# Whole fp32 operands in the experts' one-hot matmuls, and an overflow loop that prepares each block one block ahead

## The chip, the cores and the metric

The kernel runs on one core of a Trainium2 chip. The metric is the time of one execution on the device in microseconds. Times of a kernel are compared as medians of several runs; the profile shows one more execution, with every instruction of the five engines: PE (TensorE, matmuls; its weight loads are shown apart as PEld), DVE (VectorE), ACT (ScalarE), POOL (GpSimd) and SP (SyncE, which here issues nearly all DMAs).

## The reference, cut to what matters

The trunk has two layers. Each mixes 512 tokens of width 1024 by three mixers, attends to 256 memory tokens, and ends in a mixture of 32 experts, of which each token takes two:

```python
def hierarchical_moe(x, ...):
    g_p, g_idx = lax.top_k(softmax(t @ w_group + b_group), 1)
    e_p, e_idx = lax.top_k(softmax(e_logits[token, g_idx]), 2)
    weights = g_p * e_p / sum(e_p)
    expert_id = g_idx * 8 + e_idx
    gate = sum(one_hot(expert_id, 32) * weights)
    for e in range(32):
        h = silu(t @ w_gate[e]) * (t @ w_up[e])
        out = out + (h @ w_down[e]) * gate[:, e:e + 1]
    return out
# x = layer_norm(ALPHA * x + hierarchical_moe(x, ...), ln3_g, ln3_b)
```

All values are fp32. The change touches only the mixture of experts.

## The kernel before

The tokens lie in four tiles of 128 (t = 0 to 3). An expert has 64 slots (CAP), and experts are worked in pairs p = 0 to 15, so a pair fills 128 rows. Only the tokens that chose a pair's experts are worked: a one-hot matrix with a 1 where a token has a slot picks them.

**Two forms of an fp32 matmul.** A matmul whose operands are fp32 as they stand is compiled to two instructions on PE, which the trace shows as two records. An operand that `split` (L355 to L357) has cut into a high and a low half of type fp32r (ACT copies the high half, DVE subtracts it to get the low one) is multiplied by one record for each half. A one-hot matrix needs no low half.

**Router.** `router_tile` (L1158) runs once for each token tile at the end of the memory attention's output projection: layer norm, transposes, logits (L1178, L1179), the choice of experts on DVE (L1182 to L1199), then the split of the tile into the two halves X[0], X[1] (L1201 to L1205), the rank of each token among those of its expert (PE L1207 to L1209, the last of them needing the DVE result `rM` of L1199), its slot (DVE L1211 to L1214) and the one-hot rows of the first two pairs (L1219, L1220). Four more matmuls (L1251) serve the gates.

**First gather.** `gather_first` (L1329) gathers the tokens of pairs 0 and 1: for each tile t and each of eight column blocks f, two matmuls of 256 columns (L1340), one for each half. Later pairs get their tokens from DRAM by an indirect DMA (`fetch` on POOL) and eight transposes (`fetched`, L1325).

**The loop over pairs** in `moe` (L1421). Each turn issues on PE, by hand-written order, first the `down` matmuls of the pair before (L1395) and the `up` matmuls of this one (L1372), both with whole fp32 operands of 64 columns each, and then four pieces, each made of transposes for the next pair (L1325, in the first two pieces), token tables (L1304) or the turn of the hidden values (L1385), followed by two calls of `scatter`. `scatter` (L1513) adds a pair's results to the tokens: for each tile t and half of the width hf two matmuls of 512 columns (L1518), with the two halves y[0] and y[1] of the result, and one DVE addition (L1522). y[0] is made by ACT (L1397) from the down product, y[1] by DVE (L1398). So a pair has 8 calls of `scatter` and 16 records. There are 16 sets of scatter in a layer: the first, while pair 1 is under way; 14 in the later turns; and one in the tail.

**The tail.** After the last pair its two halves of down and scatter follow, now with sums for the last norm (L1524). In layer 0 filler matmuls of the next layer (tile `fb`, L393 to L395) are mixed in.

**Overflow.** Tokens beyond an expert's 64 slots are worked in blocks by a loop whose count is known only at run time (L1564, L1565). Here it runs no block in layer 0 and one block in layer 1. In a block, POOL compares all slots (L1538, eight instructions), adds (L1539) and PE finds the tokens (L1542), the weights (L1549) and the transposed one-hot rows (L1554); POOL then fetches the tokens by an indirect DMA (L1315), PE transposes them (L1325), and up (L1581), down (L1594) and scatter (L1603, DVE L1604) follow. SP loads the block's weights (L1571). After the loop comes `last_norm` (L1616).

## Time and profile before

| what | value |
|---|---|
| median of 3 runs | 1554.85 us (1550.07 to 1559.25) |
| the profiled execution's own time | 1561.04 us |
| its span in the trace | 1559.24 us |
| PE busy | 1478.3 us, 95% of the span |
| DVE busy | 1054.6 us, 68% |
| ACT busy | 592.0 us, 38% |
| POOL busy | 88.3 us, 6% |
| scatter matmuls L1518 | 512 records, 153.4 us |
| first gather L1340 | 128 records |
| read from HBM | 307.88 MB |

A row of a timeline gives the start, the duration, the engine, line and operation, tile names, the shape (rows x columns), and how many like instructions it stands for; brackets hold the idle time before it and what ended that. Matmuls overlap in the pipeline, so the spacing of starts is the price of a matmul in a stream, not the duration of one. Durations are those of the one profiled execution.

### The profile page before, as it was taken

Reading aid. Unit: us, or ns where it says so; the run is one execution under the profiler, and the core shown is the slowest. Engines: PE = TensorE matmul, PEld = TensorE weight load, DVE = VectorE, ACT = ScalarE, POOL = GpSimd, SP = SyncE. Lnnn points to the kernel's source line nnn. Section 1 sums busy time; section 2 is a strip of 40 time slices with the busy share of each in tenths; the row PEclk is TensorE's granted clock in tenths of the full one; section 3 lists DMA queues with packets and bytes.
Section 4 is the critical chain, followed back from the end, with each engine's and each line's share of the span. In section 5 each row is a group of like instructions: output and inputs, shape, how many; then the busy total and the mean of one; then the engine's idle time right before and its main releaser. Section 6 shows DMA issues by size and latency. Waiting matters only on the chain. (4 is left out here: it accounts for less than half of the span.)

```text
span 1559.2 us, 22997 instructions
## 1 busy us (share of the span) xinstructions
PE 1478.3 (95%) x8646; PEld 1011.7 (65%) x8646; DVE 1054.6 (68%) x2316; ACT 592.0 (38%) x1137; POOL 88.3 (6%) x102
## 2 busy tenths in 40 slices
PE   8999999999998999999799999999999999999984
PEld 6788876788785344444578878658887844444432
DVE  6868678576467986454856867786664699755454
ACT  6544346425333232332463342562442333323212
POOL 0000000010000011110000000000000011111010
PEclk9999899999999999999899999999999999999996
DMA  6432220413437999996533322014225589999931
GB/s 227 143 129 82 89 75 21 167 63 108 138 126 273 414 412 413 413 411 279 171 128 109 110 102 75 28 66 158 82 95 174 203 332 413 413 413 413 411 136 55
DMA packets 95909, 314.53 MB, mean 202 GB/s; under 512 B 12820, under 2 KB 13332, under 8 KB 95668
## 3 DMA queue, kind: packets, MB, share of 16 engines
q1 hardware_dynamic: 90532, 301.36, 51.8%
q0 software_dynamic: 4112, 7.48, 1.3%
q10 hardware_dynamic: 1152, 4.19, 0.7%
q8 instruction: 69, 1.13, 0.3%
q14 instruction: 44, 0.36, 0.1%
HBM read 307.88 MB, written 12.58 MB: 206 GB/s over the span
## 5 line engine op out<-in xcount | busy, mean ns | idle before, releaser
L357 DVE TENSOR_TENSOR wlo<-raw,whi 128x1024 fp32r<-128x1024 f32 x86 | 104.7, 1221 | 87.2 <-ACT whi L356 86.9
L1518 PE MATMUL sm<-e_y,e_oT 128*128 128x512 f32 x512 | 153.4, 422 | 7.7 <-ACT T L1350 2.9
L1522 DVE TENSOR_TENSOR e<-e,sm 128x512 f32<-128x512 f32 x240 | 149.8, 682 | 10.5 <-PE sm L1518 10.1
L393 PE MATMUL pj<-T,whi 128*128 128x512 f32 (+1 forms) x368 | 137.3, 374 | 6.5 <-ACT T L356 5.4
L356 ACT CAST whi<-raw 128x1024 fp32r<-128x1024 f32 x86 | 89.9, 1049 | 129.2 <-PE sm L394 52.0
L394 PE MATMUL pj<-T,wlo 128*128 128x512 f32 (+1 forms) x368 | 137.0, 373 | 1.9 <-DVE wlo L357 1.9
L395 PE MATMUL pj<-T,whi 128*128 128x512 f32 (+1 forms) x368 | 136.3, 371 | 0.0
L1518 PEld LDWEIGHTS sm<-e_y,e_oT 128*128 128x128 f32 x512 | 85.0, 189 | 43.8 <-ACT e_hT L1387 8.6
L393 PE MATMUL pj<-whi,T 128*128 128x512 f32 (+1 forms) x272 | 105.1, 386 | 5.5 <-ACT T L859 5.2
L395 PE MATMUL pj<-wlo,T 128*128 128x512 f32 (+1 forms) x272 | 104.1, 385 | 0.8 <-DVE wlo L357 0.8
L394 PE MATMUL pj<-whi,T 128*128 128x512 f32 (+1 forms) x272 | 104.0, 382 | 0.0
L1397 ACT ACTIVATE e_y<-pj,rws 128x512 fp32r<-128x512 f32 x64 | 43.8, 687 | 130.6 <-PE pj L1395 114.7
L1372 PE MATMUL pj<-e,T 128*64 128x512 f32 x376 | 92.3, 596 | 0.0
L1380 DVE TENSOR_TENSOR e_sl<-e_sl,pj 128x256 f32<-128x256 f32 x32 | 13.5, 421 | 115.5 <-ACT e_sl L1379 115.4
L1350 ACT ACTIVATE T<-sm,vec 128x128 f32<-128x128 f32 (+2 forms) x236 | 85.9, 467 | 5.1 <-PE sm L1325 5.1
L1372 PE MATMUL pj<-T,T 128*64 128x512 f32 x384 | 85.5, 592 | 0.0
L393 PEld LDWEIGHTS pj<-T,whi 128*128 128x128 f32 x368 | 71.8, 195 | 18.9 <-ACT T L356 6.9
L1379 ACT ACTIVATE e_sl<-pj 128x256 f32<-128x256 f32 x32 | 12.3, 383 | 184.4 <-PE pj L1372 184.4
L394 PEld LDWEIGHTS pj<-T,wlo 128*128 128x128 f32 x368 | 71.7, 195 | 13.6 <-DVE wlo L357 2.8
L395 PEld LDWEIGHTS pj<-T,whi 128*128 128x128 f32 x368 | 71.6, 195 | 11.4 <-issue 0.9
L1398 DVE SCALAR_TENSOR_TENSOR e_y<-pj,rws,e_y 128x512 fp32r<-128x512 f32 x64 | 47.8, 749 | 36.1 <-ACT e_y L1397 36.0
L356 ACT CAST fwh<-fw 128x512 fp32r<-128x512 f32 x60 | 37.2, 620 | 90.3 <-PE fb L394 36.2
(499 smaller groups left out, 3230.1 us busy)
## 6 DMA issues: line engine op xcount, KB each, us to landing
T<-in_gu SPq DMA_DIRECT2D x96, 512.0 KB, 10.8
raw<-in_pieces SPq DMA_DIRECT2D x94, 512.0 KB, 3.4
e<-in_gu SPq DMA_DIRECT2D x94, 512.0 KB, 10.0
T<-in_dn SPq DMA_DIRECT2D x48, 512.0 KB, 10.5
e<-in_dn SPq DMA_DIRECT2D x34, 512.0 KB, 10.0
whi<-in_gu SPq DMA_DIRECT2D x32, 512.0 KB, 10.4
fw<-in_pieces SPq DMA_DIRECT2D x60, 256.0 KB, 3.0
raw<-in_dn SPq DMA_DIRECT2D x24, 512.0 KB, 9.9
```

The source lines that it names most:

```text
L356: self.nc.scalar.copy(hi, src)
L357: self.nc.vector.tensor_tensor(lo, src, hi, op=OP.subtract)
L393: mm(ps, a[0], b[0], start=first, stop=False)
L394: mm(ps, a[1], b[0], start=False, stop=False)
L395: return mm(ps, a[0], b[1], start=False, stop=last)
L1350: self.nc.scalar.activation(Xs[:, f, :], ps, AF.Identity, scale=v[:, VC_LG + f:VC_LG + f + 1], bias=v[:, VC_LB + f:VC_LB + f + 1])
L1372: run.append(nc.tensor.matmul(st["h"][CAP * i:CAP * i + CAP, :], Xs[:, k, i * CAP:(i + 1) * CAP], st["w"][i][:, (k % 2) * 512:(k % 2 + 1) ...
L1380: nc.vector.tensor_tensor(sl[0:R], sl[0:R], st["h"][0:R, DE:], op=OP.mult)
L1397: nc.scalar.activation(y[0][0:R, c], po[0:R, :], AF.Copy, scale=ws)
L1398: nc.vector.scalar_tensor_tensor(y[1][0:R, c], po[0:R, :], ws, y[0][0:R, c], op0=OP.mult, op1=OP.subtract)
L1518: m = nc.tensor.matmul(ps, ohT[:, t * P:(t + 1) * P], y[i][0:n, c], start=i == 0, stop=i == 1)
L1522: nc.vector.tensor_tensor(x[t][:, c], x[t][:, c], ps, op=OP.add)
```

## The change

Gather, scatter and overflow scatter take whole fp32 operands: the one-hot tiles (`oh`, `e_oT`) and the result `e_y` become fp32, each pair of half matmuls becomes one matmul, and the splits of X and the low half y[1] are gone, with X's two large tiles.

The overflow block is cut in two. `overflow_next` compares the slots, finds tokens and weights in one product (two columns instead of one, so no separate L1549) and fetches the rows. It is called once ahead of the tail, in both layers, whether a block follows or not, and again within each turn of the loop for the block after. `overflow_block` transposes the rows that are there already and makes the transposed one-hot rows by a DVE comparison, without PE.

```diff
@@ router_state / router_tile @@
-        X = [self.t([P, NT, D], "T16", 4, F32R, self.tp) for _ in range(2)]
-        r["X"] = [[z[:, t, :] for t in range(NT)] for z in X]
-        r["oh0"] = self.t([P, NT, 256], "oh", 2, F32R, self.mp)
+        r["oh0"] = self.t([P, NT, 256], "oh", 2, pool=self.mp)
...
-        chosen = tt(M[:, t, :], oh[0], oh[1], op=OP.add)
-        if t == NT - 1:
-            with self.tc.issue_after(chosen.ins):
-                self.split(r["X"][0][t], r["X"][1][t], x)
-        else:
-            self.split(r["X"][0][t], r["X"][1][t], x)
+        tt(M[:, t, :], oh[0], oh[1], op=OP.add)
@@ gather_first @@
-                for i in range(2):
-                    nc.tensor.matmul(ps, X[i][t][:, f * P:(f + 1) * P], oh[:, t, :], start=False,
-                                     stop=f % 2 == 1 and i + t == NT)
+                nc.tensor.matmul(ps, x[t][:, f * P:(f + 1) * P], oh[:, t, :], start=False, stop=f % 2 == 1 and t == NT - 1)
@@ down @@
-                y.extend(self.t([P, D], "e_y", 2, F32R, self.mp) for _ in range(2))
+                y.append(self.t([P, D], "e_y", 2, pool=self.mp))
...
-            nc.vector.scalar_tensor_tensor(y[1][0:R, c], po[0:R, :], ws, y[0][0:R, c], op0=OP.mult, op1=OP.subtract)
@@ moe, ahead of the tail @@
+        o = self.overflow_tiles(l, r)
+        self.overflow_next(l, r, o)
@@ scatter @@
-        for i in range(2):
-            m = nc.tensor.matmul(ps, ohT[:, t * P:(t + 1) * P], y[i][0:n, c], start=i == 0, stop=i == 1)
+        m = nc.tensor.matmul(ps, ohT[:, t * P:(t + 1) * P], y[0][0:n, c], start=True, stop=True)
@@ new @@
+    def overflow_tiles(self, l, r):
+        nc = self.nc
+        o = {"o2": self.t([P, 2, NT, 2, CAP], "oh", 2, pool=self.mp), "rows": self.t([P, D], "oh", 2, pool=self.mp)[0:CAP],
+             "id": self.t([P, 2], "mid"), "ix": self.t([P, 1], "mox", dt=I32), "ws": self.t([P, 1], "mow"),
+             "tw": self.t([P, 2, NT, 2], "mtw")}
+        for j in range(2):
+            nc.gpsimd.tensor_copy(o["tw"][:, j, :, 0], self.tok)
+            nc.gpsimd.tensor_copy(o["tw"][:, j, :, 1], r["w"][:, :, j])
+        return o
+    def overflow_next(self, l, r, o):
+        nc, so = self.nc, r["s2"]
...
+        for j in range(2):
+            for t in range(NT):
+                nc.gpsimd.tensor_scalar(o["o2"][:, j, t], io, so[:, t, j:j + 1], None, op0=OP.is_equal)
+        nc.gpsimd.tensor_scalar(so, so, float(-CAP), None, op0=OP.add)
+        ps = self.bank()
+        for j in range(2):
+            for t in range(NT):
+                nc.tensor.matmul(ps[:, 0:2], o["o2"][:, j, t].rearrange("p a b -> p (a b)"), o["tw"][:, j, t], start=j + t == 0,
+                                 stop=j + t == NT)
+        nc.vector.tensor_scalar(o["ix"], ps[:, 0:1], float(FARTOK), None, op0=OP.add)
+        for i in range(2):
+            nc.vector.tensor_scalar(o["id"][:, i:i + 1], ps[:, 0:1], float(FARTOK - 256 * i), None, op0=OP.add)
+        nc.vector.tensor_copy(o["ws"], ps[:, 1:2])
+        nc.gpsimd.memset(o["rows"], 0.0)
+        nc.gpsimd.indirect_dma_start(o["rows"], None, self.ud[l], bass.IndirectOffsetOnAxis(ap=o["ix"][0:CAP], axis=0),
+                                     bounds_check=T - 1, oob_is_err=False)
+    def overflow_block(self, l, r, o):
+        Xs, ohT = self.t([P, KC, CAP], "T16", 4, pool=self.tp), self.t([P, T], "e_oT", 2, pool=self.mp)
+        for g in range(2):
+            self.fetched(l, Xs, o["rows"], g, [])
+        for i in range(2):
+            self.nc.vector.tensor_scalar(ohT[:, 256 * i:256 * i + 256], self.c("iota"), o["id"][:, i:i + 1], None, op0=OP.is_equal)
+        ws = self.t([P, 1], "mow2")
+        self.nc.vector.tensor_copy(ws, o["ws"])
+        return Xs, ws, ohT
@@ overflow, in the loop @@
-            Xs, ws, ohT = self.overflow_block(l, r)
+            Xs, ws, ohT = self.overflow_block(l, r, o)
+            self.overflow_next(l, r, o)
...
-                    for v in y:
-                        nc.tensor.matmul(ps, ohT[rows, t * P:(t + 1) * P], v[rows], start=v is y[0], stop=v is y[1])
+                    nc.tensor.matmul(ps, ohT[rows, t * P:(t + 1) * P], y[rows], start=True, stop=True)
```

The lines move: in the changed file the gather is L1332, the transposes L1318, the ranks L1201 and L1202, up L1363, down L1386, scatter L1509, the slot comparison L1535, the token and weight product L1540, and the overflow's up, down and scatter L1583, L1596 and L1603.

On PE, in a turn of the loop (the last but one pair of layer 1), before:

```order
L1325 MATMUL sm_13586<-const,oh_13399 128x128 x4
L1518 MATMUL sm_13595<-e_y_13527,e_oT_13464 128x512
L1518 MATMUL sm_13595<-e_y_13528,e_oT_13464 128x512
L1518 MATMUL sm_13599<-e_y_13527,e_oT_13464 128x512
L1518 MATMUL sm_13599<-e_y_13528,e_oT_13464 128x512
L1325 MATMUL sm_13603<-const,oh_13399 128x128 x4
```

and now:

```order
L1318 MATMUL sm_13195<-const,oh_13022 128x128 x4
L1509 MATMUL sm_13204<-e_y_13139,e_oT_13084 128x512
L1509 MATMUL sm_13207<-e_y_13139,e_oT_13084 128x512
L1318 MATMUL sm_13210<-const,oh_13022 128x128 x4
L1509 MATMUL sm_13219<-e_y_13139,e_oT_13084 128x512
```

The places are the same; each bank `sm` gets one whole matmul instead of one for each half.

On PE, at the end of the router of layer 1, around the last tile's rank (`rM` with `sut`), before (`T_2124` and `T_2125` are the halves of X):

```order
L1340 MATMUL sm_11537<-oh_10978,T_2124_10968 128x256
L1340 MATMUL sm_11537<-oh_10978,T_2125_10969 128x256
L1208 LDWEIGHTS sut_108
L1208 MATMUL sm_10967<-rM_10974,sut_108 128x32
L1209 LDWEIGHTS ones_104
L1209 MATMUL sm_10967<-e_110,ones_104 128x32
L1251 LDWEIGHTS ones_104
L1251 MATMUL sm_10967<-rM_10974,ones_104 128x32
```

and now (`e_1907` is tile 2 of the tokens, `e_1908` tile 3):

```order
L1201 MATMUL sm_10764<-rM_10769,sut_108 128x32
L1202 LDWEIGHTS ones_104
L1202 MATMUL sm_10764<-e_110,ones_104 128x32
L1332 MATMUL sm_11324<-oh_10773,e_1906_9647 128x256
L1332 MATMUL pj_11321<-oh_10773,e_1907_9648 128x256 x2
L1332 MATMUL pj_11322<-oh_10773,e_1907_9648 128x256 x2
L1332 MATMUL pj_11323<-oh_10773,e_1907_9648 128x256 x2
L1332 MATMUL sm_11324<-oh_10773,e_1907_9648 128x256 x2
L1332 MATMUL pj_11321<-oh_10773,e_1908_9649 128x256 x2
```

Before, all matmuls of the first three tiles stood ahead of the last tile's rank, and behind it, after L1251, the 16 of the last tile; now the whole of tile 2 and one of tile 1 stand there too, 17 whole matmuls in all.

On DVE at the same place, the last tile's norm (`rnm`) among the choice and the slots of tile 2 (`rei` to `oh`), before:

```order
L461 TENSOR_SCALAR ln_ve_11469<-ln_mv_11467 128x1
L1190 MAX rem_10971<-res_11416 128x8
L1166 SCALAR_TENSOR_TENSOR rnm_11473<-ln_mv_11467,ln_rs_11470 128x1
L1191 MAX_INDEX rei_11408<-rem_10971,res_11416 128x8
L1193 CAST ref_11421<-rei_11408 128x2
```

and now:

```order
L461 TENSOR_SCALAR ln_ve_11258<-ln_mv_11256 128x1
L1207 SCALAR_TENSOR_TENSOR rh_11222,rs_10772<-roh_2109_10768,rV_10771 128x32
L1212 TENSOR_SCALAR oh_10773<-const,rs_10772 128x256
L1164 SCALAR_TENSOR_TENSOR rnm_11262<-ln_mv_11256,ln_rs_11259 128x1
L1213 SCALAR_TENSOR_TENSOR oh_10773<-const,rs_10772,oh_10773 128x256
```

The norm's step `rnm` has moved from ahead of tile 2's choice (L1191) to behind the first of its one-hot instructions (L1212, L1219 before).

On PE, in the overflow loop of layer 1, before:

```order
L1542 MATMUL sm_13860<-tok,e_y_13850 128x1 x4
L1549 MATMUL sm_13872<-rw_11704,e_y_13849 128x1 x8
L1554 MATMUL sm_13882<-const,e_y_13850 128x128 x4
L1325 MATMUL sm_13889<-const,oh_13867 128x64 x4
L1325 MATMUL sm_13898<-const,oh_13867 128x64 x4
L1581 MATMUL pj_13907<-raw_13834,T_2774_13846 64x256 x4
```

and now:

```order
L1318 MATMUL sm_13463<-const,oh_13337 128x64 x4
L1318 MATMUL sm_13472<-const,oh_13337 128x64 x4
L1540 MATMUL sm_13494<-mtw_13341,oh_13336 128x2 x8
L1583 MATMUL pj_13511<-raw_13449,T_2745_13461 64x256 x4
L1583 MATMUL pj_13511<-whi_13451,T_2745_13461 64x256 x4
```

The transposes come first, and the product L1540 for the block after stands between them and the up matmuls; the same eight stand once more ahead of the tail's first down.

## Rows read from the trace of the kernel before

**Rows 1.** Busy time by stretch; last three: granted clock, DMA share, GB/s.
```profile
522.80:636.10 113.30, 112.31 (x544) 50.77 (x542) 88.51 (x202) 35.19 (x84) 13.62 (x14) 1.00 1.03 413
...
1205.00:1247.30 42.30, 38.48 (x277) 34.23 (x275) 27.20 (x129) 14.98 (x21) 2.94 (x5) 1.00 0.54 194
...
1512.30:1532.10 19.80, 13.57 (x72) 10.10 (x71) 2.85 (x10) 3.06 (x10) 8.03 (x12) 0.66 0.37 139
```

**Rows 2.** Timeline of PE, one turn of the loop over pairs, layer 0.
```profile
620.22 2.31 PE L1372 MATMUL pj<-e,T 128*64 128x512 f32 x9
...
627.19 0.66 PE L1325 MATMUL sm<-const,oh 128*128 128x128 f32 x4
627.60 1.17 PE L1518 MATMUL sm<-e_y,e_oT 128*128 128x512 f32 x4
628.61 0.60 PE L1325 MATMUL sm<-const,oh 128*128 128x128 f32 x4
629.09 2.24 PE L1518 MATMUL sm<-e_y,e_oT 128*128 128x512 f32 x8
631.17 0.38 PE L1385 MATMUL sm<-const,e_sl 128*128 128x128 f32 x2
631.31 1.44 PE L1518 MATMUL sm<-e_y,e_oT 128*128 128x512 f32 x4
632.68 0.64 PE L1395 MATMUL pj<-whi,e_hT 128*64 128x512 f32 x1
...
636.16 0.60 PE L1372 MATMUL pj<-T,T 128*64 128x512 f32 x2
```

**Rows 3.** Timeline of PE: two half matmuls, streaming, in layer 1's projection.
```profile
1213.20 0.39 PE L394 MATMUL pj<-whi,T 128*128 128x512 f32 x1
1213.43 0.39 PE L395 MATMUL pj<-wlo,T 128*128 128x512 f32 x1
```

**Rows 4.** Timeline: one whole fp32 matmul (two records) of the same shape.
```profile
233.48 1.02 PE L622 MATMUL sm<-K,Q 128*128 128x512 f32 x2
```

**Rows 5.** Waits of PE's weight loads, 530 to 740 us: total, times, longest.
```profile
PEld sm L1518 <- ACT e_hT L1387: 3.9, 9, 0.5
PEld sm L1518 <- DVE e L1522: 3.5, 13, 0.5
...
PEld pj L1395 <- DMA T<-in_gu: 1.9, 6, 0.4
```

**Rows 6.** Timeline of DVE and PE, end of layer 1's router.
```profile
1229.57 1.21 DVE L357 TENSOR_TENSOR T<-e,T 128x1024 fp32r<-128x1024 f32 x1
...
1232.90 0.16 DVE L1166 SCALAR_TENSOR_TENSOR rnm<-ln_mv,ln_rs 128x1 f32<-128x1 f32 x1 [0.65 <-POOL ln_rs L462]
...
1235.83 0.49 DVE L1220 SCALAR_TENSOR_TENSOR oh<-const,rs,oh 128x256 fp32r<-128x256 f32 x1
...
1242.53 0.18 PE L1208 MATMUL sm<-rM,sut 128*128 128x32 f16 x1 [0.69 <-DVE rM L1199]
...
1245.35 1.65 PE L1340 MATMUL pj<-oh,T 128*128 128x256 f32 x12 [1.12 <-DVE oh L1220]
...
1246.83 0.63 PE L1340 MATMUL sm<-oh,T 128*128 128x256 f32 x4
```

**Rows 7.** Timeline of DVE: end of layer 0's loop, which runs no block.
```profile
759.40 0.33 DVE L1632 TENSOR_SCALAR lst<-lsum 128x1 f32<-128x1 f32 x2 [1.73 <-issue]
```

**Rows 8.** Timeline, all engines: layer 1's tail and overflow block.
```profile
1511.08 2.14 PE L1518 MATMUL sm<-e_y,e_oT 128*128 128x512 f32 x8 [0.78 <-ACT e_y L1397]
...
1512.48 4.67 POOL L1538 TENSOR_SCALAR e_y<-const,rs 128x128 f32<-128x128 f32 x8 [56.99 <-PE sm L1518]
...
1519.33 1.87 PE L1542 MATMUL sm<-tok,e_y 128*128 128x1 f32 x8 [6.11 <-POOL e_y L1539]
...
1526.68 1.98 PE L1581 MATMUL pj<-raw,T 128*64 128x256 f32 x8
...
1531.02 1.03 PE L1581 MATMUL pj<-whi,T 128*64 128x256 f32 x8
...
1537.85 0.69 DVE L1604 SCALAR_TENSOR_TENSOR e<-sm,e 128x512 f32<-128x512 f32 x1 [0.58 <-PE sm L1603]
```

More of the change, by code (lines that the diff above doesn't have):

```diff
@@ L1327, in fetched, with gather_first @@
             self.gathered(l, Xs, 4 * g + k, ps[:, k * n:(k + 1) * n])
-    def gather_first(self, l, Xs, oh, X):
+    def gather_first(self, l, Xs, oh, x):
         nc, v = self.nc, self.vec[l]
@@ L1419, in fill_ahead, with moe @@
         self.fill = self.memory(l, range(self.n_gap), self.load_memT(page), page, lambda: self.t([P, T], "e_s", 4, pool=self.mp))
-    def moe(self, l, r, X, x, following):
+    def moe(self, l, r, x, following):
         nc, a = self.nc, self.a
@@ L1429, in moe @@
         oh16 = XX[:, 3].bitcast(F16).rearrange("p (i t s) -> p i t s", i=2, t=NT)
-        add = self.gather_first(l, first, r["oh0"], X)
+        add = self.gather_first(l, first, r["oh0"], x)
         for t in range(NT):
@@ L1488, in moe @@
                 self.scatter(x, y, ohT, t, hf, sums[:, t, hf:hf + 1])
-        self.overflow(l, r, x, sums)
+        self.overflow(l, r, x, sums, o)
         return self.last_norm(x, gb, sums)
@@ L1494, in onehot_rows @@
         nc = self.nc
-        ohT, junk = self.t([P, T], "e_oT", 2, F32R, self.mp), self.t([P, T], "e_j", 1, F16, self.mp)
+        ohT, junk = self.t([P, T], "e_oT", 2, pool=self.mp), self.t([P, T], "e_j", 1, F16, self.mp)
         pi, w2 = self.c("pidx")[:, p:p + 1], self.t([P, 2], "ew2", 2)
@@ L1516, in scatter @@
         ps, c, n = self.bank(), slice(hf * 512, (hf + 1) * 512), ohT.shape[0]
-        for i in range(2):
-            m = nc.tensor.matmul(ps, ohT[:, t * P:(t + 1) * P], y[i][0:n, c], start=i == 0, stop=i == 1)
-            if run is not None:
-                run.append(m)
+        m = nc.tensor.matmul(ps, ohT[:, t * P:(t + 1) * P], y[0][0:n, c], start=True, stop=True)
+        if run is not None:
+            run.append(m)
         if total is None:
@@ L1537, in overflow_block @@
             for t in range(NT):
-                nc.gpsimd.tensor_scalar(o2[:, j, t], io, so[:, t, j:j + 1], None, op0=OP.is_equal)
-        nc.gpsimd.tensor_tensor(oh, o2[:, 0], o2[:, 1], op=OP.add)
-        ps = self.bank()
-        for t in range(NT):
-            nc.tensor.matmul(ps[:, 0:1], oh[:, t].rearrange("p a b -> p (a b)"), self.tok[:, t:t + 1], start=t == 0, stop=t == NT - 1)
-        ix = self.t([P, 1], "mox", dt=I32)
-        nc.vector.tensor_scalar(ix, ps[:, 0:1], float(FARTOK), None, op0=OP.add)
-        rows = self.fetch(l, ix, CAP)
+                nc.gpsimd.tensor_scalar(o["o2"][:, j, t], io, so[:, t, j:j + 1], None, op0=OP.is_equal)
+        nc.gpsimd.tensor_scalar(so, so, float(-CAP), None, op0=OP.add)
         ps = self.bank()
@@ L1548, in overflow_block, with overflow @@
             for t in range(NT):
-                nc.tensor.matmul(ps[:, 0:1], o2[:, j, t].rearrange("p a b -> p (a b)"), r["w"][:, t, j:j + 1],
-                                 start=j + t == 0, stop=j + t == NT)
-        nc.vector.tensor_copy(ws, ps[:, 0:1])
-        ps = self.bank()
-        for t in range(NT):
-            nc.tensor.transpose(ps[:, t * P:(t + 1) * P], oh[:, t].rearrange("p a b -> p (a b)"), self.ident)
-        nc.scalar.copy(ohT, ps)
-        nc.gpsimd.tensor_scalar(so, so, float(-CAP), None, op0=OP.add)
-        for g in range(2):
-            self.fetched(l, Xs, rows, g, [])
+                nc.tensor.matmul(ps[:, 0:2], o["o2"][:, j, t].rearrange("p a b -> p (a b)"), o["tw"][:, j, t], start=j + t == 0,
[9 more added lines that the diff above has]
+        Xs, ohT = self.t([P, KC, CAP], "T16", 4, pool=self.tp), self.t([P, T], "e_oT", 2, pool=self.mp)
+        for g in range(2):
+            self.fetched(l, Xs, o["rows"], g, [])
[3 more added lines that the diff above has]
+        self.nc.vector.tensor_copy(ws, o["ws"])
         return Xs, ws, ohT
-    def overflow(self, l, r, x, sums):
+    def overflow(self, l, r, x, sums, o):
         nc, a, ebi = self.nc, self.a, r["ebi"]
@@ L1595, in overflow @@
                                      start=k == 0, stop=k == 1)
-            y = [self.t([P, D], "e_y", 2, F32R, self.mp)[:, 0:512] for _ in range(2)]
-            nc.scalar.activation(y[0], po, AF.Copy, scale=ws)
-            nc.vector.scalar_tensor_tensor(y[1], po, ws, y[0], op0=OP.mult, op1=OP.subtract)
+            y = self.t([P, D], "e_y", 2, pool=self.mp)[:, 0:512]
+            nc.scalar.activation(y, po, AF.Copy, scale=ws)
             for t in range(NT):
@@ L1698, in layer @@
         r = self.router_state(l)
-        X = r["X"]
         self.proj_residual(l, PI_XO, oT, x, None, lambda t, st, gb: self.router_tile(x[t], t, st, r),
@@ L1702, in layer @@
         last = l == L - 1
-        x = self.moe(l, r, X, x, None if last else l + 1)
+        x = self.moe(l, r, x, None if last else l + 1)
         if not last:
```

6 lines of the change are left out of this document (removed).

## The prediction

> **What bounds the kernel now.** I read the busy time by stretch first, then one turn of the loop over pairs, then the router and the tail. In the first long stretch of layer 0's pair loop PE is busy for 112.31 of 113.30 us at the full granted clock, while DVE has 88.51 and ACT 35.19 [rows 1]. DMA is close behind: 1.03 of its capacity, 413 GB/s. Which of the two ends last is told by PE's waits: its weight loads wait for weights from DMA six times, 1.9 us in all, in 210 us of loop [rows 5]. So the weights arrive ahead of their use, and PE sets the pace. Whatever adds PE time to a turn adds it to the kernel, 28 times over. Work that the change takes from ACT and DVE in a turn is worth nothing there.
>
> One turn runs from the first up matmul at 620.22 to the next at 636.16, 15.94 us [rows 2]. Between 627.19 and 632.68, 5.49 us, stand transposes, turn and scatter. The two groups of four transposes take .41 and .48 us from their start to the next row, the turn .14. That leaves 4.46 us for the sixteen half matmuls of scatter.
>
> At the end of the router the bound is another: the last tile's rank waits for DVE (.69 us, 1242.53) and its gather waits 1.12 us for the one-hot row [rows 6]. PE is busy for 38.48 of 42.30 us there [rows 1]. In layer 1's overflow block nothing streams: PE has 13.57 of 19.80 us, at a mean clock of .66 of full speed [rows 1].
>
> **Price of the two forms.** Two half matmuls of 512 columns in a stream start .23 us apart [rows 3], so a call of scatter costs .46. One whole fp32 matmul of the same shape leaves two records, together 1.02 us [rows 4]. A lone whole record of 512 columns lasts .60 in the loop (636.16) [rows 2]; 1.02 less that is .42 between the starts. The up matmuls, two at a time side by side, give .43 (nine records in 2.31 us: 2.31 less .60, over four steps) [rows 2]. I take .43, so .86 for a whole matmul, 1.87 times the two halves. At 256 columns, which no row shows for the whole form, I halve this: .43 a matmul, against 2 x .12 for halves (twelve records from 1245.35 to 1246.83) [rows 6].
>
> The Trainium skill says of true fp32 that it takes "4 passes through PE array" (FP8 and Floating Point Precision, TensorE Precision Notes), and that matmuls of 512 columns follow each other at 215.7 ns when warm (TensorE: Matmul & The Clock Gate, Part 2). That speaks against this change: two halves are two passes and the whole form is four. An estimate from these two pages is .863 us whole and .431 for the halves. The row agrees on the first (.86) and puts the second at .46. By the pages the 28 turns would cost 28 x 8 x .431 = 96.6 us; the sum below goes by the rows.
>
> **A. Scatter in the loop.** Eight whole matmuls are 6.88 us in place of 4.46. If every wait and every uncovered weight load among the sixteen goes under, a turn grows by 2.42. If all that is above 16 x .23 = 3.68, which is .78, stays, it grows by 3.20. PE's waits at scatter are for DVE's additions and ACT's copies, 3.5 and 3.9 us in 22 cases, at most .5 each [rows 5]; a slower PE gives both more time, so some of the .78 goes, but transposes with fresh banks still end in a short wait. I take 2.7. There are 14 such turns in each layer: 28 x 2.7 = **+75.6**. The first set of each layer runs while pair 1 still waits for its tokens, so it costs between 0 and 3.2; 1.5 each, **+3.0**.
>
> **B. Gather and router.** Before, the last tile's rank starts at 1242.53 and its sixteen half matmuls end at 1246.83 + 4 x .12 = 1247.3, 4.8 us later, the wait of 1.12 within [rows 6]. Now 17 whole matmuls stand behind the rank. Nine of them belong to earlier tiles; at .43 they take 3.9 us, which covers the 2.8 us that DVE needs from the rank to the one-hot row. Eight follow, 3.4 us. With .2 for the rank this is 7.5, so +2.7. The rank itself: the norm of the last tile stood at 1232.90 and now waits for DVE's chain of tile 2, which ended with the row at 1235.83, 2.9 us later; in exchange the split at 1229.57, 1.21 us, is gone from ahead of it [rows 6]. Its net is between 0 and +1.7; I take 1.0, since a part of the chain to the rank ran with idle time. 3.7 for each layer, **+7.4** (bounds 2 to 5 each).
>
> **C. Tail of layer 0.** The product L1540 is sixteen records ahead of the first down. No record of that form is in the trace; the nearest are the transposes, whole fp32 of 128 columns, .41 us for four [rows 2], so 1.65 us at full clock. Each half's scatter goes from 8 x .23 = 1.84 to 4 x .86 = 3.44, +1.6; PE waits .78 for ACT's result ahead of the second half (layer 1's row) [rows 8], so 1.5 each is enough. All three together are 4.65. Against that, the filler matmuls and their splits, which now delay this scatter, can move behind it. Between 0 and 4.65; I take **+2.0**. POOL's compares for this needless preparation lie beside the pair loop, and POOL holds up nothing that PE waits for there.
>
> **D. Tail of layer 1.** Again 1.65 + 2 x 1.5 = +4.65. From the end of the scatter (1511.08 + 2.14 = 1513.2) to the end of up (1531.02 + 1.03 = 1532.05) there are now 18.85 us: eight compares on POOL (4.67), the addition, then products at 1519.33 that take 1.87 for eight records, fetch, transposes, up [rows 8]. After the change the fetched rows are there before the loop. What is left: entering the loop, for which layer 0 gives a bound of 1.73 (entering and leaving) [rows 7], 1.2 taken; eight transposes, .8; ACT's first copies, .4; L1540 for the next block, 1.65; up, which took 1532.05 - 1526.68 = 5.37 at a mean clock of .66 of the stretch [rows 1], so 3.5 at full clock. Together 7.55, which saves 11.3; 11 taken. At the slow level (.23 a record for L1540, 5.4 for up) it saves 7, with no time for entering 12.5. The low half of the block's y also leaves the path ahead of the first addition at 1537.85 [rows 8], -.5. POOL's compares for the next block wait only for the product ahead of the tail, so they run during the tail. **-7** (bounds -9 to 0).
>
> **Sum.** 75.6 + 3.0 + 7.4 + 2.0 - 7 = +81.0. The profiled execution took 1561.04 us, so 1642.0 for it; it lies 6.2 above the median of the runs shown, 1554.85, which gives **1636**.
>
> **Rivals.**
>
> 1. *A whole record costs what a half record costs.* Both forms leave the same number of records, and if the record set the price, scatter would cost nothing more. A is then 0, B only the +1.0 of the rank in each layer, C about 1, and D 4.65 - 3.0 - 11.5 = -9.9: 2 + 1 - 9.9 = -7, so 1548, on the other side. It decides below a price of about .244 us a record (7 us over 512 records of scatter above .23). Rows 4 and the up matmuls say .43; what speaks for it is only that row 4 is a single case. 3 in 100.
>
> 2. *PE's waits go under altogether.* If the .78 a turn is all wait for DMA, DVE and ACT, the turn grows by 2.42, the first set by nothing; 67.8 + 0 + 5 + 1 - 9 = +65, 1620. For it: DMA is at 1.03 of its capacity, so a slower PE would meet no late weights. Against: PE's waits for weights are 1.9 us in 210. 15 in 100.
>
> 3. *No wait goes under.* Weight loads of whole operands stay uncovered as now: 28 x 3.2 = 89.6, first sets 3, router 9, tails 4 and -4: +102, 1656. For it: fewer, longer matmuls between waits of the same kind. 15 in 100.
>
> 4. *The overlapped preparation fails.* L1540 for the next block stands ahead of up on PE. If POOL reaches the loop only with the others, its 4.67 us of compares end at 1513.2 + 1.2 + 4.7, two microseconds after up would start, and if PE falls to its slower level (1.2 in place of 2.4 GHz) meanwhile, 4 more go: D = -1, 1642. 10 in 100.
>
> **How the numbers follow.** My forecast has 57 in 100, the rivals 3, 15, 15 and 10. Only the first is not slower. The range takes in all of rivals 2 and 4 and the near part of 3: 1619 to 1653. What a measurement of this kernel can tell from no change is about .5%, 8 us; faster by more .02, within it .02, slower .96.
>
> **What would show it.** Scatter's records should start .43 apart instead of .23, with as many records as now; a turn of the loop should be 18.6 us instead of 15.94, at a DMA share near .87. Gather should end about 7.5 us after the last rank. In layer 1's loop the transposes should start within 2 us of the last scatter, and up should end some 7.5 us after it. The prediction is wrong if the whole record's spacing in scatter is under .4, if other work in the turn speeds up because PE is fuller, or if PE is granted less than its full clock in the loop.

## The result and the profile after

The changed kernel takes 1624.50 us (median of 4 runs, 1621.19 to 1632.88) against 1556.51 us for the kernel before (4 runs, 1550.07 to 1559.25). The ratio is 1.0451, 95% interval 1.0395 to 1.0507: the change costs 68 us, between 61 and 79. The profiled execution took 1627.70 us, its span is 1625.63 us.

Part 1 of the page after, busy time and share of each engine, and from part 5 the row of the scatter matmuls (busy time, mean ns of one, idle time ahead of them):

```profile
PE 1566.9 (96%) x8666; PEld 1017.3 (63%) x8666; DVE 1016.9 (63%) x2256; ACT 586.4 (36%) x1128; POOL 102.8 (6%) x131
...
L1509 PE MATMUL sm<-e_y,e_oT 128*128 128x512 f32 x512 | 238.7, 596 | 0.9 <-ACT e_y L1388 0.8
```

There are as many scatter records as before, 512, and their busy time went from 153.4 to 238.7 us, by 85; PE's whole busy time went from 1478.3 to 1566.9, by 89. DVE lost 38 us of work and ACT 6; in the loop, where PE sets the pace, none of that came back.

Two windows of equal content, the last nine turns of layer 0's pair loop, in the kernel before and after (length, then busy time of PE, PEld, DVE, ACT and POOL with their counts, then granted clock, DMA share and GB/s). Before:

```profile
588.16:732.17 144.01, 143.64 (x693) 65.09 (x691) 77.71 (x136) 45.24 (x108) 13.63 (x14) 1.00 0.99 397
```

and after:

```profile
595.00:762.96 167.96, 167.96 (x693) 66.04 (x691) 66.29 (x110) 46.23 (x108) 19.46 (x24) 1.00 0.84 319
```

PE has the same 693 instructions; it is idle for .37 us before and without a gap now, and a turn has grown from 16.00 to 18.66 us. DMA, at .99 before, is at .84 now: the weights wait for PE, not PE for the weights. The waits of PE's weight loads agree: between 530 and 740 us those put down to DMA were 9.6 us in 32 cases and are 1.8 in 6 now. Those of the scatter's loads for DVE and ACT were 8.5 us in 25 cases (two rows of them in [rows 5]) and are 1.7 in 7, of which this is the longest row:

```profile
PEld sm L1509 <- DVE e L1513: 1.0, 4, 0.2
```

One turn of this loop on PE, which answers to [rows 2]:

```profile
620.53 0.66 PE L1318 MATMUL sm<-const,oh 128*128 128x128 f32 x4
621.02 1.88 PE L1509 MATMUL sm<-e_y,e_oT 128*128 128x512 f32 x4
622.74 0.60 PE L1318 MATMUL sm<-const,oh 128*128 128x128 f32 x4
623.18 1.88 PE L1509 MATMUL sm<-e_y,e_oT 128*128 128x512 f32 x4
624.90 0.34 PE L1297 MATMUL sm<-tok,T 128*128 128x1 f16 x8
625.10 1.96 PE L1509 MATMUL sm<-e_y,e_oT 128*128 128x512 f32 x4
626.90 0.38 PE L1376 MATMUL sm<-const,e_sl 128*128 128x128 f32 x2
627.12 1.88 PE L1509 MATMUL sm<-e_y,e_oT 128*128 128x512 f32 x4
628.93 3.65 PE L1386 MATMUL pj<-e,e_hT 128*64 128x512 f32 x16
```

Four records of scatter take 1.72 us from their start to the next row (621.02 to 622.74), .43 a record. Four half records took 1.01 there [rows 2], .25 each.

The end of layer 1's router on PE, which answers to [rows 6]:

```profile
1277.32 0.18 PE L1201 MATMUL sm<-rM,sut 128*128 128x32 f16 x1
...
1277.55 0.70 PE L1332 MATMUL sm<-oh,e 128*128 128x256 f32 x2
1278.08 2.75 PE L1332 MATMUL pj<-oh,e 128*128 128x256 f32 x12
...
1284.12 1.03 PE L1332 MATMUL sm<-oh,e 128*128 128x256 f32 x4
```

From the last tile's rank to the end of the gather there are 7.8 us (1284.12 + 1.03 less 1277.32), without one wait, where there were 4.9 with two (1.17 us for DVE's `rV` and the 1.12 of [rows 6]).

The tail of layer 1 and the overflow block, which answer to [rows 8]:

```profile
1580.18 4.67 POOL L1535 TENSOR_SCALAR oh<-const,rs 128x128 f32<-128x128 f32 x8
...
1587.29 3.70 PE L1509 MATMUL sm<-e_y,e_oT 128*128 128x512 f32 x8 [0.78 <-ACT e_y L1388]
...
1590.92 0.71 PE L1318 MATMUL sm<-const,oh 64*128 64x64 f32 x8
...
1591.55 1.95 PE L1540 MATMUL sm<-mtw,oh 128*128 128x2 f32 x16
...
1593.43 1.56 PE L1583 MATMUL pj<-raw,T 128*64 128x256 f32 x8
...
1597.76 1.03 PE L1583 MATMUL pj<-whi,T 128*64 128x256 f32 x8
```

POOL's compares for the block after run during the tail, the transposes of the block start as the last scatter ends (1587.29 + 3.70), and up ends 7.8 us after it (1597.76 + 1.03), where it took 18.8 before.

Stretch by stretch, from positions in the two traces (and in a second profile of the kernel before, which is one of the experiments), with what the prediction gave to each:

| stretch | before | before again | after | predicted | measured |
|---|---|---|---|---|---|
| start to layer 0's last rank | 480.34 | 478.63 | 477.61 | 0 | -2.7 |
| last rank to pair 1's up, layer 0 | 23.99 | 22.93 | 23.22 | +3.7 | -0.8 |
| turn with the first scatter set | 18.50 | 18.30 | 19.32 | +1.5 | +0.8 |
| 13 turns, layer 0 | 209.33 | 209.41 | 242.80 | +35.1 | +33.5 |
| last up to the last norm, layer 0 | 27.24 | 27.22 | 33.84 | +4.7 | +6.6 |
| last norm to layer 1's last rank | 483.13 | 482.08 | 480.54 | 0 | -2.6 |
| last rank to pair 1's up, layer 1 | 21.43 | 21.42 | 23.22 | +3.7 | +1.8 |
| turn with the first scatter set | 18.67 | 17.38 | 18.86 | +1.5 | +0.2 |
| 13 turns, layer 1 | 209.44 | 209.33 | 242.80 | +35.1 | +33.4 |
| last up to the end of the pairs' scatter | 21.16 | 21.12 | 28.79 | +7.4 | +7.6 |
| to the end of the block's up | 18.83 | 19.53 | 7.81 | -11 | -11.0 |
| to the end | 27.19 | 26.73 | 26.84 | -.5 | -.3 |
| sum | 1559.24 | 1554.09 | 1625.63 | +81 | +66.4 |

The fourteenth set of each layer is in the row of the last up. The two long stretches with a predicted 0 differ in every profile that was taken: together they take between 952 and 963 us in ten profiles, and the first profile of before has the longest. So the column on the right, which is taken against that profile, flatters the change by some of the 5.3 us in these two rows; what it costs is told by the medians.

### The profile page after: what moved, and what is told of

Same layout as the page of the kernel before. It is cut to its first block, busy times and chain, and to the rows that moved or that the text cites. A ratio compares the mean times of both kernels' runs of the same rounds, so it can differ in the third digit from the quotient of the medians.

```text
span 1625.6 us, 23053 instructions
## 1 busy us (share of the span) xinstructions
PE 1566.9 (96%) x8666; PEld 1017.3 (63%) x8666; DVE 1016.9 (63%) x2256; ACT 586.4 (36%) x1128; POOL 102.8 (6%) x131
## 5 line engine op out<-in xcount | busy, mean ns | idle before, releaser
L1509 PE MATMUL sm<-e_y,e_oT 128*128 128x512 f32 x512 | 238.7, 596 | 0.9 <-ACT e_y L1388 0.8
L1513 DVE TENSOR_TENSOR e<-e,sm 128x512 f32<-128x512 f32 x240 | 163.7, 686 | 55.1 <-PE sm L1509 54.5
L1509 PEld LDWEIGHTS sm<-e_y,e_oT 128*128 128x128 f32 x512 | 89.1, 190 | 78.2 <-issue 69.8
L1388 ACT ACTIVATE e_y<-pj,rws 128x512 f32<-128x512 f32 x64 | 43.8, 687 | 157.7 <-PE pj L1386 141.7
L1363 PE MATMUL pj<-e,T 128*64 128x512 f32 x376 | 89.3, 593 | 0.0
L1363 PE MATMUL pj<-T,T 128*64 128x512 f32 x384 | 85.5, 592 | 0.0
L1363 PEld LDWEIGHTS pj<-e,T 128*64 128x64 f32 x376 | 28.4, 137 | 56.0 <-issue 53.7
## 6 DMA issues: line engine op xcount, KB each, us to landing
T<-in_dn SPq DMA_DIRECT2D x48, 512.0 KB, 10.2
e<-in_dn SPq DMA_DIRECT2D x34, 512.0 KB, 10.2
```

The costliest lines, as they stand in the source:

```text
L1363: run.append(nc.tensor.matmul(st["h"][CAP * i:CAP * i + CAP, :], Xs[:, k, i * CAP:(i + 1) * CAP], st["w"][i][:, (k % 2) * 512:(k % 2 + 1) ...
L1388: nc.scalar.activation(y[0][0:R, c], po[0:R, :], AF.Copy, scale=ws)
L1509: m = nc.tensor.matmul(ps, ohT[:, t * P:(t + 1) * P], y[0][0:n, c], start=True, stop=True)
L1513: nc.vector.tensor_tensor(x[t][:, c], x[t][:, c], ps, op=OP.add)
```

## The experiments

**Only the scatter whole.** The theory: the pairs' scatter carries more than the whole loss, by PE's time alone.

```diff
-        for i in range(2):
-            m = nc.tensor.matmul(ps, ohT[:, t * P:(t + 1) * P], y[i][0:n, c], start=i == 0, stop=i == 1)
+        m = nc.tensor.matmul(ps, ohT[:, t * P:(t + 1) * P], y[0][0:n, c], start=True, stop=True)
```

(with y and the one-hot rows of the pairs as fp32 and y's low half gone; all else as before)

> The kernel before with only the pairs' scatter on whole fp32 operands; the gather, the overflow block and its scatter stay as they were. Theory (PE time in the loop carries the loss, and nearly all short waits among the scatter records go under): 28 turns longer by 2.57 us each = 72, the first sets 2, the four tail halves 1.6 each = 6.4, together +80 us against before, so more than the whole change costs. Rival (part of the loss sits in the gather and router): +60 to +68. Rival (the waits stay): 28 x 3.2 + 9 = +99.

Measured: 1624.03 us against 1554.69, ratio 1.0438 (1.0415 to 1.0461), +69 us, between 65 and 72. This is 11 under the theory and just above the rival that the theory was set against (+60 to +68); the medians alone would have settled on the wrong story. The trace shows where most of the 11 went. The thirteen turns are 242.80 us in each layer, to the hundredth what the whole change has. So the loop carries all that the theory gave it. What was not foreseen is in the overflow block, which this edit leaves as it was. POOL and PE there:

```profile
1570.15 4.68 POOL L1536 TENSOR_SCALAR e_y<-const,rs 128x128 f32<-128x128 f32 x8 [58.16 <-PE sm L1516]
...
1579.03 3.70 PE L1516 MATMUL sm<-e_y,e_oT 128*128 128x512 f32 x8 [0.78 <-ACT e_y L1397]
...
1582.91 1.26 POOL L1537 TENSOR_TENSOR e_y<-e_y 128x512 f32<-128x512 f32 x1 [7.19 <-PE sm L1516]
...
1584.23 1.05 PE L1540 MATMUL sm<-tok,e_y 128*128 128x1 f32 x8 [1.50 <-POOL e_y L1537]
```

The compares start at 1570.15, 8.9 us before the second half's scatter, and not 1.4 us after its start as in [rows 8]. Their target is one of the two `e_y` buffers, and in both kernels a scatter is named as the releaser. Before, the last pair's two halves fill both buffers, so the compares start within the tail's own second scatter. Here its one result fills one, and they start .2 us behind the scatter of the pair before (it ends at 1569.95). The next experiment is a control: it lengthens the scatter as well but keeps the low half, and there the compares start 1.4 us after the scatter's start again, and the block takes 19.0 us. So the longer scatter is not what moves them; the buffer fits, though it was not tried by itself. From the end of the scatter to the end of up there are 13.2 us in place of 18.8, 5.6 us back that have nothing to do with the form of a matmul. The stretch up to layer 0's last rank, whose code does not differ, was 7.6 us shorter in this execution than in the first profile of before, and 5.9 shorter than in the second. The scatter's own loss, against the first profile of before, is .6 + .2 for the first sets, 33.5 + 33.4 for the turns and 4.9 + 5.9 for the tails with their fourteenth sets, +78.4 us, and 1.5 more against the second. So the theory's +80 stands for what it spoke of, in the one execution that was profiled. The block's 5.6 leaves +73 of it; that the medians have +69 may lie in the unchanged stretches, which no profile of the other three executions shows.

**Three half records.** PE's time without the fp32 form: a third record in each call, which counts the result's low half twice.

```diff
-        for i in range(2):
-            m = nc.tensor.matmul(ps, ohT[:, t * P:(t + 1) * P], y[i][0:n, c], start=i == 0, stop=i == 1)
+        for i in range(3):
+            m = nc.tensor.matmul(ps, ohT[:, t * P:(t + 1) * P], y[min(i, 1)][0:n, c], start=i == 0, stop=i == 2)
```

> The kernel before with a third half record in each call of the pairs' scatter: the low half of the result is multiplied and added twice (so the output counts it twice). Operands, DVE and ACT work stay as before; only PE has 8 records more in a set. Theory (PE's occupancy is the price, and the .78 us of waits in a turn go under when PE is slower): 24 x .23 + .1 in place of 4.46 us is +1.16 in a turn, 28 x 1.16 + 1 + 4 x .9 = +37 us. Rival (waits stay): 8 x .23 = 1.84 a turn, 28 x 1.84 + 5 = +56 us. Rival (the loss of the change comes from the fp32 form and not from PE's time): under +15 us.

Measured: 1594.09 us, ratio 1.0249 (1.0233 to 1.0266), +39 us, between 36 and 41. One turn:

```profile
635.06 0.66 PE L1325 MATMUL sm<-const,oh 128*128 128x128 f32 x4
635.47 1.63 PE L1518 MATMUL sm<-e_y,e_oT 128*128 128x512 f32 x6
636.94 0.60 PE L1325 MATMUL sm<-const,oh 128*128 128x128 f32 x4
```

Six records in 1.47 us, .245 each, where four took 1.01. The thirteen turns take 226.21 us in layer 0, 1.29 a turn more than in the second profile of before, near the 1.16 of the theory and far from the 1.84 of the rival that the waits stay. ACT and DVE have the same instructions as before, so the loop pays for PE's time without the fp32 form too.

**Only the gather whole.** This tests the term that the first comparison of the traces had made doubtful.

```diff
-                for i in range(2):
-                    nc.tensor.matmul(ps, X[i][t][:, f * P:(f + 1) * P], oh[:, t, :], start=False,
-                                     stop=f % 2 == 1 and i + t == NT)
+                nc.tensor.matmul(ps, x[t][:, f * P:(f + 1) * P], oh[:, t, :], start=False, stop=f % 2 == 1 and t == NT - 1)
```

(and the split of X gone; scatter and overflow as before)

> The kernel before with only the first gather on whole fp32 operands and the split of X gone. Prediction's term B: the last rank 1.0 later and the gather 2.7 longer behind it, +3.7 in each layer, +7.4 us. Theory after the trace: the last rank is not later, because the split is gone from DVE's chain; the gather is 2.9 longer behind it, but the first up matmuls and the first turn wait less, so +0 to +1.5 in each layer, 0 to +3 us in all. Rival (all of PE's added time shows): 32 x .43 - 64 x .12 = 6 in each layer, +12 us.

Measured: 1559.78 us (10 runs) against 1554.69 (23 runs), ratio 1.0037 (1.0017 to 1.0058), +5.1 us, between 2.6 and 9. Both what the prediction gave and, at its upper end, the theory after the trace lie within that; +12 does not. Against the second profile of before, the trace has +.3 and +1.8 us from the last rank to pair 1's up in the two layers, and +1.2 and +1.2 in the turn with the first scatter set. That turn varies by itself (17.4 to 18.9 us in the profiles of kernels with halves in it), so how much of the second pair is the gather's is open. The profiled execution was also the fastest of the ten (1553.76 us), so its trace can't show where the 5.1 lies. The last rank is not later: from the first tile's rank to the last tile's it takes 27.25 us in both layers, and 27.23 and 27.24 in the kernel before.

**Only the overflow pipelined.**

```diff
+        o = self.overflow_tiles(l, r)
+        self.overflow_next(l, r, o)
         self.filler("x0")
...
-            Xs, ws, ohT = self.overflow_block(l, r)
+            Xs, ws, ohT = self.overflow_block(l, r, o)
+            self.overflow_next(l, r, o)
```

(with the new functions of the change; all one-hot matmuls on halves)

> The kernel before with only the overflow loop pipelined: preparation ahead of the tail in both layers, all one-hot matmuls on halves. Theory: in layer 1 the up of the block starts 11 us sooner after the last scatter, the product ahead of each tail costs 1.75 on PE in both layers: -11 + 3.5 = -7.5 us (-9 to -5), up itself no faster. Rival (without the longer scatter the prepared rows come too late, or POOL's compares for the next block hold the product ahead of up): -3 to 0 us.

Measured: 1549.61 us (12 runs), ratio .9961 (.9935 to .9986), -6 us, between -10 and -2. The theory's value is inside. This half of the change is a gain by itself. From the end of the scatter to the end of up it takes 8.6 us, 10.2 less than before; up is no faster than before:

```profile
1516.54 1.92 PE L1551 MATMUL sm<-mtw,oh 128*128 128x2 f32 x16 [0.24 <-DVE e L1526]
...
1518.38 1.69 PE L1594 MATMUL pj<-raw,T 128*64 128x256 f32 x8
...
1522.71 1.03 PE L1594 MATMUL pj<-whi,T 128*64 128x256 f32 x8
```

Up takes 5.4 us (1518.38 to 1523.74), as it did before. The tail cost 1.6 us more in layer 1, as the theory has it, but 3.7 more in layer 0. There the product is followed by a stretch at the slow level: five down records take 2.76 us, which take 1.45 at the same place of the changed kernel.

**The kernel before, profiled again.** No edit; it tells what belongs to the run and what to the kernel.

> The kernel before, profiled once more. Theory (the low granted clock between 165 and 176 us of the first profile, .54 there, has nothing to do with the change): this profile shows the full clock there or somewhere else in the first 450 us, and the low clock at the layer boundary (about 760 to 780 us) and in layer 1's overflow block (about 1512 to 1532 us) again, since PE idles there. Rival (the low clock sits at fixed places of this program): the same stretches at the same level.

The span is 1554.09 us. Windows of the first profile of before, and then of this one:

```profile
165.00:176.00 11.00, 11.00 (x108) 8.47 (x108) 4.79 (x9) 2.90 (x6) 0.00 (x0) 0.54 0.29 100
```

```profile
165.00:176.00 11.00, 11.00 (x141) 9.07 (x140) 7.84 (x16) 4.58 (x9) 0.00 (x0) 1.00 0.36 121
760.00:780.00 20.00, 14.68 (x73) 12.41 (x73) 17.12 (x21) 11.14 (x18) 2.48 (x4) 0.70 0.69 236
1507.80:1527.40 19.60, 13.37 (x69) 10.05 (x68) 2.23 (x10) 3.06 (x9) 7.34 (x11) 0.65 0.33 126
```

In the same 11 us, with PE busy throughout in both, one execution had a clock of .54 and 108 instructions, the other 1.00 and 141. The layer boundary and the overflow block are low in both. So the theory holds (in the first profile the boundary's 760 to 780 us are at .64): some stretches at the slow level belong to a place where PE idles, and some come and go with the execution. Against this profile the changed kernel's span is 71.5 longer, against the first one 66.4.

**Dummy matmuls in the overflow block.**

```diff
+        ps = self.bank()
+        for _ in range(24):
+            nc.tensor.matmul(ps, self.zero16, self.zero16[:, 0:1].to_broadcast([P, 512]), start=True, stop=True)
```

> The kernel before with 24 dummy matmuls of zeros (128x512, 16 bit) on PE at the start of the overflow block, where PE waits for POOL's compares. They add PE work, nothing uses their result. Theory (the block is slow because the granted clock falls while PE idles): the products L1542, L1549 and the up matmuls run at the full clock, eight products in about .9 us in place of 1.87, up in 3.5 in place of 5.4, and from the last scatter of the pairs to the end of up it takes 14 to 17 us in place of 18.9. Rival (other causes): 18.9 us or more.

```profile
1502.54 5.38 PE L1534 MATMUL sm<-zero 128*128 128x512 f16 x24
1508.58 1.05 PE L1545 MATMUL sm<-tok,e_y 128*128 128x1 f32 x8 [0.66 <-POOL e_y L1542]
1509.49 2.58 PE L1552 MATMUL sm<-rw,e_y 128*128 128x1 f32 x16
...
1514.64 1.97 PE L1584 MATMUL pj<-raw,T 128*64 128x256 f32 x8
...
1518.62 1.03 PE L1584 MATMUL pj<-whi,T 128*64 128x256 f32 x8
```

The eight products went from 1.87 us [rows 8] to 1.05, as the theory has it. But the products L1552 and up (5.0 us) were not carried along: the clock of the stretch is .80, the slow level came back among the one-column products. From scatter to the end of up it took 17.2 us in place of 18.8, just outside what the theory gave. This is one execution (1548.19 us), and its total tells nothing here, since the unchanged stretch from layer 0's last norm to layer 1's last rank was 8.3 us shorter than in the first profile of before. The same block takes 18.5 to 19.5 us in the four other profiles whose block starts its compares as before. So the idle time of PE is part of why this block is slow, 1.3 to 2.3 us here, and keeping PE busy only ahead of it does not cure it.

**The changed kernel without layer 0's preparation.**

```diff
-        self.overflow_next(l, r, o)
+        if not following:
+            self.overflow_next(l, r, o)
         self.filler("x0")
```

> The changed kernel without the preparation ahead of layer 0's tail (layer 0 has no overflow block, so nothing needs it). Theory (the product's 16 records stand openly on PE): layer 0's tail, from the end of the last up to the first instruction of the last norm, is 1.8 us shorter than in the changed kernel. Rival (it hides beside ACT and DVE work): under .5 us.

From the end of the last up to the first instruction of the last norm, layer 0 takes 25.11 us in place of 26.80: 1.7 less. The sixteen records of the product stand openly on PE; nothing hides them (one execution, 1624.95 us).

The trace shows one thing more. Layer 1's block is the same code as in the changed kernel, with the same sixteen records ahead of up, and here up ran at the full clock:

```profile
1590.70 1.95 PE L1541 MATMUL sm<-mtw,oh 128*128 128x2 f32 x16
1592.58 1.08 PE L1584 MATMUL pj<-raw,T 128*64 128x256 f32 x8
...
1595.22 1.03 PE L1584 MATMUL pj<-whi,T 128*64 128x256 f32 x8
```

It took 3.7 us (1592.58 to 1596.25) in place of 5.4, and 6.1 from the end of the scatter to its end in place of 7.8.

**Halves, pipelined, with a cheaper product.**

```diff
-        o = {"o2": self.t([P, 2, NT, 2, CAP], "oh", 2, pool=self.mp), "rows": self.t([P, D], "oh", 2, pool=self.mp)[0:CAP],
+        o = {"o2": self.t([P, 2, NT, 2, CAP], "oh", 2, F16, self.mp), "rows": self.t([P, D], "oh", 2, pool=self.mp)[0:CAP],
...
-             "tw": self.t([P, 2, NT, 2], "mtw")}
+             "tw": self.t([P, 2, NT, 3], "mtw", dt=F16)}
...
+            nc.gpsimd.tensor_copy(o["tw"][:, j, :, 1], r["w"][:, :, j])
+            nc.gpsimd.tensor_tensor(o["tw"][:, j, :, 2], r["w"][:, :, j], o["tw"][:, j, :, 1], op=OP.subtract)
...
+            with self.tc.issue_after(mm.ins):
+                self.overflow_find(l, o)
```

(the edit is against the kernel of "only the overflow pipelined"; `overflow_find` is the part of `overflow_next` from the product on, and is called behind `overflow_next` ahead of the tail; `mm` is the last up matmul of the block)

> All one-hot matmuls of gather and scatter on halves as before; overflow pipelined as in the changed kernel, but with the product for tokens and weights on 16-bit operands (the weight as a high and a low part, three columns), 8 records in place of 16, and, in the loop, issued behind the block's up matmuls. Theory: the product costs about .6 us in place of 1.75 in each tail and nothing ahead of up, so 2 x 1.1 + 1.9 = 4 us less than pipelining alone (which measured -6): -8 to -12 us against before. Rival (the product hides, or its place doesn't matter): -6 us.

Measured: 1541.70 us (9 runs) against 1554.76 (14 runs), ratio .9922 (.9898 to .9947), -12 us, between -8 and -16. It beats both kernels, and the changed one by 83 us. The block:

```profile
1506.64 2.10 PE L1521 MATMUL sm<-e_y,e_oT 128*128 128x512 f32 x8 [0.78 <-ACT e_y L1397]
...
1509.86 1.08 PE L1600 MATMUL pj<-raw,T 128*64 128x256 f32 x8
...
1513.35 1.08 PE L1600 MATMUL pj<-whi,T 128*64 128x256 f32 x8 [0.20 <-DMA whi<-in_gu]
1514.37 0.35 PE L1556 MATMUL sm<-mtw,oh 128*128 128x3 f16 x8
```

The product takes .35 us in place of 1.95, and the tails are only .2 us longer than before, less than the theory's .6 each. Up runs at the full clock, 1.08 for eight records, and now ends 5.7 us after the scatter; between its parts it waits .23 and .20 us for its weights. The edit makes the product cheaper and moves it behind up, and the two were not tried apart. That up is at the full clock is not shown to be their doing: the experiment before this one has it with the old product ahead of up.

## Why the prediction was right, and where it was off

The sign, the cause and the range were right; the size was 81 against 68, and several terms were off.

**A, the loop: right, a little high.** A turn grew by 2.57 us where I took 2.7 between 2.42 and 3.20. The price of a whole record, .43, was read rightly from [rows 4]. The 2.57 lies halfway between my 2.7 and rival 2's 2.42, because more waits go under than I took: in the turn shown, the 8.40 us from 620.53 to 628.93 less .49 and .44 for transposes, .20 for tokens and .22 for the turn leave 7.05, against 8 x .86 = 6.88, so .17 of the .78 is left there. One reading of mine was too narrow: the six waits for DMA, 1.9 us, are the longest row alone, and all rows of that window come to 9.6 us in 32 cases. PE was busy nonetheless, so the conclusion stands, but rival 2, against which I held this number, looked weaker than it was. The 26 turns counted in the table give 66.8 of the 70.2 predicted. The 28 turns, the fourteenth at the same price, make 72. The extra half record of the second experiment went the same way.

The Trainium skill says of true fp32 that it takes four passes (FP8 and Floating Point Precision, TensorE Precision Notes), and gives 215.7 ns from one matmul of 512 columns to the next (TensorE: Matmul & The Clock Gate, Part 2). The estimate from both was .863 us for a whole matmul, and the trace agrees, .86; for two halves it was .431, and there the trace has .46 to .50. By it the 28 turns would have cost 96.6 us; they cost 72, since the halves were dearer and most of the waits among them went under.

**First sets: somewhat high.** 1.0 us in all against the first profile of before and 2.5 against the second, where I had 3.0; inside the bounds given.

**B, gather and router: the step that failed.** I had two parts. That 17 whole matmuls behind the rank take 7.5 us was right: 7.8. That the rank itself comes 1.0 later was wrong. The norm of the last tile did move behind the chain of tile 2 on DVE, as the order showed, but that chain runs sooner, since the split ahead of it is gone: tile 2's rank came 6.8 us behind tile 1's, where it was 9.3 before. In the profile after it stands at 1266.25, .5 us behind the first zeroing matmul, and before it stood 3.7 us behind it (1230.60 to 1234.31). In the profile after:

```profile
1265.77 0.39 PE L1327 MATMUL pj<-zero 128*128 128x512 f16 x1
1266.25 0.18 PE L1201 MATMUL sm<-rM,sut 128*128 128x32 f16 x1
```

So nothing was late: from the first tile's rank to the last tile's it takes 27.24 us in layer 1 before and 27.25 after. I had also stopped at the end of the gather. From there to the end of the first pair's up matmuls it took 8.3 us and now takes 7.2, which gives 1.1 back. The trace shows where: before, six matmuls of the token tables stand on PE behind the first up matmul, so that one runs alone for 1.0 us instead of beside its partner; after, all eight stand ahead of up. Before:

```profile
1247.44 1.07 PE L1372 MATMUL pj<-e,T 128*64 128x512 f32 x2
1248.44 0.30 PE L1304 MATMUL sm<-tok,T 128*128 128x1 f16 x6
```

and after:

```profile
1284.99 0.34 PE L1297 MATMUL sm<-tok,T 128*128 128x1 f16 x8
1285.26 7.09 PE L1363 MATMUL pj<-e,T 128*64 128x512 f32 x32
```

Layer 1 paid 1.8 in place of 3.7. In layer 0 the clock hides the price. From the last rank to pair 1's up every profile with the whole gather (three kernels, both layers) takes 23.2 us at a clock of 1.00, while the kernels with halves take 21.4 at 1.00 and 22.7 to 24.1 at .86 to .93. In layer 0 all profiles with halves are among the latter, those of before with .86 and .93, which leaves -.8 and +.3; what the gather would have cost there at an equal clock is not shown. The experiment with the gather alone leaves its price at 2.6 to 9 us, part of which may lie in the turn behind it.

**C, layer 0's tail: low by 2.** 6.6 with the fourteenth set, where I had 2.7 + 2.0. I had given the filler matmuls 2.65 us of credit for moving out of the way. The seventh experiment shows that the product's 1.7 us is paid in full. The scatter's two halves cost 2.3 of the 3.0 (4.9 in the first experiment, less 2.57 for the fourteenth set), so .7 is all that the credit can have been.

**D, layer 1's tail and block: the total was right, in part by luck.** The tail cost 7.6 of 7.4, the block gave back 11.0 of 11. Two of its parts were wrong and cancelled in this execution. Entering the loop took nothing (transposes at 1590.92, scatter's end 1590.99), where I had 1.2. And up did not reach the full clock: 5.4 us as before, at a clock of .78 for the stretch from 1591.00 to 1598.80, where I had 3.5.

```profile
1591.00:1598.80 7.80, 7.79 (x56) 5.36 (x56) 2.31 (x9) 2.47 (x8) 1.95 (x2) 0.78 0.61 238
```

In the seventh experiment the same code ran at 1.00 and up took 3.7, near my 3.5; the block then gives back 12.7.

**What no term had.** 5.3 us of the difference lie in the two long stretches, whose code the change touches only at the router's end (27.2 us from the first rank to the last before, 27.3 after). The second profile of before has half of it too, 2.8. It goes with how long the clock was at its slow level in each execution: in ten profiles the stretch up to layer 0's last rank takes 472.8 to 481.4 us. The shortest (the scatter whole) and the longest (three half records) have the same 2959 PE instructions in it, and the clock makes up most of the difference, .02 of 481 us:

```profile
0.00:472.76 472.76, 453.37 (x2959) 368.31 (x2960) 332.33 (x741) 207.02 (x363) 11.63 (x16) 1.00 0.36 121
0.00:481.43 481.43, 461.05 (x2959) 373.98 (x2960) 332.61 (x741) 207.51 (x363) 11.63 (x16) 0.98 0.35 119
```

A prediction against one profiled execution carries an uncertainty of 5 us and more, and the range had to cover it.

**The rivals.** The first, that records and not columns set the price, is refuted by .43 against .25 in the same place. The second was nearer in total, 1620 against the measured 1624.5, where I had 1636; in the turn it is as far off as I am (2.42 and 2.7 against 2.57), so its nearness is in part luck. The third is refuted by the turn. Of the fourth, the part on POOL did not happen; the part on the clock did in the changed kernel's profile, at 1.7 us in place of 4, and not in the seventh experiment.

## What to carry to other kernels

Where PE is busy without a gap, price a change by the spacing of records in the trace, not by the number of instructions: a whole fp32 matmul leaves as many records as two fp32r halves and takes 1.7 to 1.9 times as long, and the work that it saves on other engines was worth nothing in such a loop here. Lean towards the end of the bounds at which the small waits of the bounding engine go under when its work grows: .17 of .78 us was left. And test the halves of a two-part change apart: the pipelined loop, hidden in a loss of 68 us, is a gain of 6 by itself (2 to 10) and of 12 (8 to 16) with its product made cheap and put behind up.

## What the runs showed that was not expected

A buffer that an edit sets free can move another engine's work by 10 us, as the releasers have it: without the low half of y, POOL's compares in the overflow block, whose target has the same two buffers, started with the tail's first down and not within its last scatter, and the block took 13.2 us in place of 18.8.

And PE was granted a slow clock not only after idle time. In the changed kernel's overflow block the up matmuls fell to the slow level behind the sixteen records of the product (L1540) on a PE that was busy for 7.79 of 7.80 us. The product alone does not decide it, though. Three kernels have it in this form (the changed one, only the overflow pipelined, and the changed one without layer 0's preparation), at eight places in all. The slow level began within .5 us behind it at three of them (this one, and layer 0's tail and the block with only the overflow pipelined) and not at the other five; and in the seventh experiment the same block ran at 1.00. So this block's code gets either level in different executions, and what decides between them is open.
